# Dilated attention, queries and keys of a head pair: two half-precision parts made before the transpose, and the transpose by DMA instead of by TensorE

## The chip, the cores and the metric

One NeuronCore of a Trainium2 chip runs the whole program. The time is device microseconds of one launch; three timed runs give a median. A separate launch is recorded by the profiler; where the text says "the profiled execution" it means that one.

## The reference, cut to what matters

The program is two layers of an encoder trunk on 1024 tokens of width 1024, in float32. Layer 0 mixes tokens by latent attention, layer 1 by dilated sliding-window attention; each ends in a squared-ReLU MLP. The change is in layer 1:

```
proj = (h @ w_in).reshape(B, S, 3 groups, 3, 16 heads, 64)
for g, (window, dilation) in enumerate(((128, 1), (512, 4), (2048, 16))):
    q = rms_norm(proj[:, :, g, 0], g_q[g]);  k = rms_norm(proj[:, :, g, 1], g_k[g]);  v = proj[:, :, g, 2]
    s = q @ k.T * 64**-0.5 + t5_bias          # only keys inside the dilated window
    o_g, lse_g = softmax(s) @ v, logsumexp(s)
o = sum over g of softmax(lse, axis=g)[g] * o_g
y = o @ w_o
```

## The kernel before, in words

The program is built twice: a fast path (`half` true) that carries each float32 operand as two float16 parts, a rounded high part and the rest, and a float32 path behind an `If` that the data of this case never takes. All that follows is the fast path. A product of two such operands is three float16 matmuls, high by high, high by low and low by high (lines 532 to 534, in `mm3`).

The dilated stage is the function `dil`. Its work is a list of 96 steps, one for each (group g, head pair pr, token-tile pair tp): 3 groups, 8 pairs of heads, 4 pairs of 128-token tiles. Eight head pairs of four steps make a group. Within a group the tokens are permuted so that a dilated window is a plain band, and when the group changes (`turn`) the permuted activations `hTp` are made by copies that are spread over the three elementwise engines (`permute`).

A step n does, in this order of the program:

- `attend` for two token tiles that are ready: `products` (line 2345) multiplies the transposed queries by the transposed keys into two PSUM banks `pss`, twelve matmuls for two tiles; `scores` adds the bias and takes the maximum on VectorE (line 2366) and the exponential on ScalarE (line 2372); the probabilities are split into two float16 parts `ph`, the high by ScalarE (line 2409), the low by VectorE for the first tile and GpSimd for the second (line 2410); then one transposing DMA on SyncE's queue turns `ph` into `pT` (line 2411), 16 blocks of 128x128 in groups 0 and 1 and 8 in group 2.
- `project`: 48 matmuls of 128x256 make queries and keys of the head pair for 256 tokens, in the bank `psproj` (lines 532 to 534).
- between the two halves of `project`, `stacks` for the queries and keys of the step two before: four float32 transposes on TensorE (line 2316) from the normed tile `qn` into a bank `psq`, then the high part by ScalarE (line 2321) and the low part by VectorE (line 2322) from PSUM into `kT`.
- `av`: probabilities by values for the tiles whose `pT` was asked for a step earlier (lines 2424 and 2425), and VectorE's reduction into `U` (line 2432).
- `qkstep`: square (ScalarE, line 2295), sum (VectorE, line 2296), the inverse root (lines 132 to 136), its fourth power on GpSimd for a later check of ranges (lines 2300 to 2302), the scaling out of PSUM into the tile `qn` on VectorE (line 2305) and the gain on the query columns on GpSimd (line 2307).

So the queries and keys of step n are normed at the end of n and the start of n+1, transposed in n+2, and first read by `products` in n+3. `kT` holds for one head pair two planes, high and low, each of 1024 key columns and 512 columns that serve as a ring of four query tiles.

SyncE's queue carries in order, besides the transposes, the weights of the next head pairs (`wqkr`, line 1968), the values (`vraw`), the bias (`bt`), and the stores of `U`. Every engine works its own list in order. The order within an engine's list is set when the program is built: a scheduler places the instructions, and matmuls keep the order of the code. PSUM has eight banks for the stage, handed out in turn. `kT` has two buffers, `qn` shares a pool of four.

The names `P`, `S` are 128 and 1024. These are the functions that the diff touches and what calls them:

Of the kernel before, what the change touches and what calls it, by code (L numbers as in the profile page):

```python
# [9 lines left out]
F32 = mybir.dt.float32  # L10
F32R = mybir.dt.float32r
F16 = mybir.dt.float16
BF16 = mybir.dt.bfloat16
I32 = mybir.dt.int32
AF = mybir.ActivationFunctionType
ALU = mybir.AluOpType
# [4 lines left out]
P = 128  # L21
D = 1024
S = 1024
# [18 lines left out]
class K:  # L42
# [2148 lines left out]
    def dil(self, at0, at1, tail, wqk, vd):  # L2191


        nc, a, tc = self.nc, self.a, self.tc
# [5 lines left out]
        D_ = lambda name, shape, dt, bufs: dpool.tile(list(shape), dt, tag=name, bufs=bufs, name=self.nm(name))  # L2200
# [88 lines left out]
        def qkstep(u, tp, ps):  # L2289

            g = u["g"]
            p8 = ps.rearrange("p (n e) -> p n e", e=64)
            sq = self.T("dsq")
            ms = self.sm("dms", 8)
            nc.scalar.activation(sq, ps, AF.Square, scale=0.125)
            nc.vector.tensor_reduce(ms, sq.rearrange("p (n e) -> p n e", e=64), op=ALU.add, axis=AX.X)
            r = self.rstd(ms, 8, "dr", self.half)
            if self.half:
                y4 = self.sm("y4", 8)
                nc.gpsimd.tensor_tensor(y4, r, r, op=ALU.mult)  # L2300
                nc.gpsimd.tensor_tensor(y4, y4, y4, op=ALU.mult)  # L2301
                nc.gpsimd.tensor_tensor(most, most, y4, op=ALU.add)
            qn = self.T("qn")
            q8 = qn.rearrange("p (n e) -> p n e", e=64)
            nc.vector.tensor_tensor(q8, p8, r.unsqueeze(2).broadcast_to([P, 8, 64]), op=ALU.mult)
            qq = qn.rearrange("p (i n e) -> p i n e", i=2, e=64)[:, :, 0:2, :]
            nc.gpsimd.tensor_tensor(qq, qq, gain[:, g : g + 1, :].unsqueeze(1).broadcast_to([P, 2, 2, 64]), op=ALU.mult)
            return qn

        def stacks(u, tp, qn):  # L2310

            ps = PS("psq")
            for k in range(2):
                for i in range(2):
                    c = i * 256 + (1 - k) * P
                    nc.tensor.transpose(ps[:, (2 * k + i) * P : (2 * k + i + 1) * P], qn[:, c : c + P], self.ident)
            s1 = 4 + tp % 2
            hi, lo = (u["k"][:, k, :].rearrange("p (s x) -> p s x", x=256)[:, tp : s1 + 1 : s1 - tp, :] for k in range(2))
            x = ps.rearrange("p (k x) -> p k x", k=2)
            if self.half:  # L2320
                nc.scalar.activation(hi, x, AF.Copy, scale=64.0)
                nc.vector.scalar_tensor_tensor(lo, x, 64.0, hi, op0=ALU.mult, op1=ALU.subtract)
            else:
                nc.scalar.activation(hi, x, AF.Copy)
                nc.vector.tensor_tensor(lo, x, hi.bitcast(F32), op=ALU.subtract)
            for i in range(2):
                c = S + (tp % 2 * 2 + i) * P
                u["q"][2 * tp + i] = u["k"][:, :, c : c + P]
# [7 lines left out]
        def window(g, t):  # L2336
            return t // 2 * 256 if g == 2 else min(max(P * t - 64, 0), S - 256)

        def products(u, t, pss, i):
            w0 = window(u["g"], t)  # L2340
            q = u["q"].pop(t)
            for n, (a, b) in enumerate(((0, 0), (1, 0), (0, 1))):
                for e in range(2):
                    r = slice(64 * e, 64 * e + 64)
                    nc.tensor.matmul(pss[e][:, i * 256 : (i + 1) * 256], q[r, a, :], u["k"][r, b, w0 : w0 + 256],
                                     start=n == 0, stop=n == 2)

        def bias_load(u, t=0):
# [196 lines left out]
        end = max(n for n, x in enumerate(steps) if x is not None)  # L2545
# [10 lines left out]
        def fetch(n):  # L2556
            for f in wtodo.pop(n, ()):
                f()

        def fetch_split(n):  # L2560
            if n in loads:
                self.held(lambda: wts.update({firsts[n][0:3]: loads.pop(n)()}))
# [51 lines left out]
        transposed, scored, ready, carry, stacking, stk, late = [], [], [], [], None, [], []  # L2614
# [6 lines left out]
        for n, step in enumerate(steps):  # L2621
# [10 lines left out]
            if step is not None:  # L2632
                kind, g, pr, tp = step
                w = wts[(kind, g, pr)]
                if tp == 0:
                    units[(g, pr)] = {"g": g, "pr": pr, "q": {}, "V": VSs[(g, pr // 2)],
                                      "k": D_("kT", (P, 2, S + 512), self.DT, 2), "U": self.G("U", (P, 8, P), F32)}
                u = units[(g, pr)]
            if self.half and step is not None and tp == 0:
                bias_load(u)  # L2640
            fetch_split(n + 1)
            transposed, scored = scored, attend(ready, n > end) if ready else []
            fetch(n)
            for u_, t_, _ in scored:
                if u_["g"] == 2:
# [5 lines left out]
            if turn:  # L2651
# [3 lines left out]
                ps = ahead.pop(0)  # L2655
            elif step is not None and ahead:
                ps = ahead.pop(0)
            elif step is not None:
                ps = PS("psproj")
# [4 lines left out]
            if len(stk) > 1:  # L2664
                x = stk.pop(0)
# [24 lines left out]
            stacking = None  # L2690
            if step is not None:
                stacking = (u, tp, qkstep(u, tp, ps))
# [200 lines left out]
```

## Time and profile before

| | us |
|---|---|
| three timed runs | 3007.45, 3010.37, 3010.95 |
| their median | 3010.37 |
| the profiled execution, its own time | 3005.26 |
| its span, first to last instruction | 3003.1 |

The profiled execution is 5.1 us below the median of the three timed runs, and 2.2 us of its time lie outside the span. The dilated stage goes from about 1548 us to about 2330 us of the span; group 0 ends near 1785, group 1 near 2043. The program also has latent attention and an MLP ahead of the stage, and an output projection and an MLP behind it, which the change leaves as they are.

How to read the rows that the prediction quotes. In a row of a timeline stand start and duration in us, the engine, the line of the program, the operation, tiles written and read, shapes and a count; what stands in brackets is idle time of the engine just before, and what ended it. PE is TensorE's matmul, PEld its weight load, DVE VectorE, ACT ScalarE, POOL GpSimd, SPq SyncE's queue of DMA issues. A matmul's duration includes its pipeline, so what a group of matmuls costs is read from start to start. In a row of the table by windows stand the length of the window, then for each engine its busy time and count, then the granted clock, the mean busy share of the 16 DMA engines and GB/s; the share can pass 1 in a short window, where packets overlap.

### The profile page before, as it was taken

The page shows a single profiled execution, that of the slowest core. Times are in us where ns is not written, and L with a number is a line of the kernel's source. Part 1 is how long each engine was busy: PE and PEld are TensorE (multiplying, and loading weights), DVE is VectorE, ACT ScalarE, POOL GpSimd, SP SyncE. Part 2 cuts the span into 40 slices and gives each one's busy share as a digit, 9 for nine tenths or more (in the row PEclk, how much of TensorE's full clock was granted, in tenths as well). Part 3 has the DMA queues.
Part 4 walks back from the last instruction along what each step waited for, and adds up shares of the span by engine and source line. Part 5 has one row for each costly group of instructions (what it writes and reads, how often), then busy time and mean ns, then how long its engine had stood idle before and what let it go on. Part 6 is the DMA issues. An engine that isn't in the chain of part 4 may idle for free. (4 is left out here: it accounts for less than half of the span.)

```text
span 3003.1 us, 54490 instructions
## 1 busy us (share of the span) xinstructions
PE 2827.4 (94%) x20148; PEld 1676.0 (56%) x20148; DVE 2251.4 (75%) x4902; ACT 1684.2 (56%) x3491; POOL 922.6 (31%) x1276
## 2 busy tenths in 40 slices
PE   6878999999999999999999989998998989999998
PEld 5634566544444444444468878876875434444443
DVE  5687777658988966788768877776886699779565
ACT  4677888825455534533238777775664355555341
POOL 6578888700211000000123344453552002110010
PEclk9999999999999999999999999999999999999999
DMA  6267455425654799546436666565656555457763
GB/s 209 72 169 161 94 117 101 131 84 188 235 188 168 251 278 289 199 159 225 171 116 148 146 139 165 145 128 117 150 129 171 144 191 210 158 186 248 238 196 86
DMA packets 589680, 503.08 MB, mean 168 GB/s; under 512 B 292277, under 2 KB 482018, under 8 KB 589402
## 3 DMA queue, kind: packets, MB, share of 16 engines
q1 hardware_dynamic: 553722, 400.74, 47.9%
q0 software_dynamic: 25248, 87.22, 7.9%
q10 hardware_dynamic: 10432, 11.54, 1.6%
q8 instruction: 159, 2.61, 0.4%
q14 instruction: 119, 0.97, 0.1%
HBM read 317.40 MB, written 125.12 MB: 147 GB/s over the span
## 5 line engine op out<-in xcount | busy, mean ns | idle before, releaser
L534 PE MATMUL psm<-hf,wf 128*128 128x512 f16 x896 | 335.8, 381 | 11.1 <-DVE wf L161 11.1
L532 PE MATMUL psm<-hf,wf 128*128 128x512 f16 x896 | 341.0, 381 | 5.0 <-ACT wf L156 5.0
L533 PE MATMUL psm<-d,d 128*128 128x512 f16 x896 | 340.8, 381 | 4.7 <-DVE d L161 4.7
L534 PE MATMUL psm<-d,d 128*128 128x512 f16 x896 | 340.7, 380 | 0.0
L533 PE MATMUL psm<-hf,wf 128*128 128x512 f16 x896 | 340.6, 380 | 0.0
L532 PE MATMUL psm<-d,d 128*128 128x512 f16 x896 | 335.0, 380 | 0.3 <-ACT d L156 0.3
L1276 POOL TENSOR_TENSOR pp<-p,pp 128x1024 f16<-128x1024 f32 x125 | 275.4, 2209 | 57.9 <-ACT pp L1269 47.8
L532 PE MATMUL psproj<-wqk,hTp 128*128 128x256 f16 x1024 | 283.0, 276 | 0.0
L533 PE MATMUL psproj<-wqk,hTp 128*128 128x256 f16 x1024 | 282.3, 276 | 0.0
L534 PE MATMUL psproj<-wqk,hTp 128*128 128x256 f16 x1024 | 282.0, 275 | 0.0
L156 ACT ACTIVATE d<-ufr 128x1024 f16<-128x1024 f32 x112 | 117.8, 1052 | 211.3 <-PE psm L534 173.3
L897 DVE TENSOR_REDUCE mx<-pmx 128x1 f32<-128x512 f32 x240 | 162.8, 687 | 78.8 <-PE pmx L895 77.4
L161 DVE SCALAR_TENSOR_TENSOR d<-ufr,d 128x1024 f16<-128x1024 f32 x112 | 136.5, 1219 | 76.5 <-ACT d L156 76.4
L1268 ACT ACTIVATE p<-pss 128x512 f32<-128x512 f32 x256 | 149.9, 590 | 43.2 <-PE pss L1259 41.8
L2372 ACT ACTIVATE pd<-pd,dnb 128x192 f32<-128x192 f32 (+2 forms) x384 | 167.3, 437 | 4.1 <-POOL y L2301 2.3
L534 PEld LDWEIGHTS <-wf 128*128 128x128 f16 x896 | 87.8, 98 | 123.3 <-DVE wf L161 19.2
L532 PEld LDWEIGHTS <-wf 128*128 128x128 f16 x896 | 87.9, 98 | 112.9 <-ACT wf L156 10.9
L534 PEld LDWEIGHTS <-d 128*128 128x128 f16 x896 | 87.9, 98 | 111.0 <-issue 6.4
L532 PEld LDWEIGHTS <-d 128*128 128x128 f16 x896 | 88.0, 98 | 106.3 <-issue 2.2
L533 PEld LDWEIGHTS <-d 128*128 128x128 f16 x896 | 87.9, 98 | 106.4 <-issue 2.5
L2410 POOL TENSOR_TENSOR ph<-pd,ph 128x512 f16<-128x512 f32 (+1 forms) x121 | 113.3, 942 | 109.3 <-ACT ph L2409 109.1
L533 PEld LDWEIGHTS <-wf 128*128 128x128 f16 x896 | 88.0, 98 | 104.9 <-issue 1.8
(439 smaller groups left out, 8122.2 us busy)
## 6 DMA issues: line engine op xcount, KB each, us to landing
ufr<-uf SPq DMA_DIRECT2D x112, 512.0 KB
w2r<-in_mlp_w SPq DMA_DIRECT2D x96, 512.0 KB
adaw<-in_ada_w SPq DMA_DIRECT2D x80, 512.0 KB
w1r<-in_mlp_w SPq DMA_DIRECT2D x64, 512.0 KB
wqkr<-in_dil_w_in SPq DMA_DIRECT2D x96, 256.0 KB
wvr<-in_dil_w_in SPq DMA_DIRECT2D x34, 512.0 KB
uf<-ub POOLq DMA_DIRECT2D x32, 512.0 KB, 3.8
uf<-ua POOLq DMA_DIRECT2D x32, 512.0 KB, 3.3
```

The lines of the kernel that those rows point to most:

```text
L156: nc.scalar.activation(hi, src, AF.Copy, scale=scale)
L161: return nc.vector.scalar_tensor_tensor(lo, src, scale, hi, op0=ALU.mult, op1=ALU.subtract, accum_out=self.seen[:, self.nseen - 1 : self.n ...
L532: mm(out, lh, rh, start=first, stop=False)
L533: mm(out, lh, rl, start=False, stop=False)
L534: mm(out, ll, rh, start=False, stop=last)
L897: nc.vector.tensor_reduce(maxes[h][:, 2 * j + b : 2 * j + b + 1], ps, op=ALU.max, axis=AX.X)
L1268: nc.scalar.activation(p[:, b * 512 : (b + 1) * 512], ps[b], AF.Exp, scale=1.0 / self.ss)
L1276: eng.tensor_tensor(q[:, 1], p, q[:, 0], op=ALU.subtract)
L2372: nc.scalar.activation(p[:, e, lo:hi], p[:, e, lo:hi], AF.Exp, scale=1.0 / self.ss, bias=nb[:, e : e + 1], accum_out=stat[:, g, t, 1, 2 * ...
L2410: (nc.gpsimd if i or u["g"] == 2 else nc.vector).tensor_tensor(lo, p, hi, op=ALU.subtract)
```

## The change

On the fast path the two parts are made where the tokens are still on the partitions, and the transpose is done on float16 by DMA:

- a new function `turned` takes the normed tile `qn` of the step just before: ScalarE copies it to float16 (line 2319 of the kernel after), GpSimd subtracts to get the low part (line 2320), both into a new tile `hl` of two buffers, whose four blocks for a token tile are query high, query low, key high, key low; then SyncE's queue issues one transposing DMA for each of the two token tiles, four blocks of 128x128 each (line 2323), straight into `kT`.
- `kT` now has four planes of 1024 columns (query high, query low, key high, key low), for all tokens of the head pair; `products` reads queries and keys from it by plane.
- the factor 64 that was applied at the two evictions moves into the scaling out of PSUM, which becomes a scalar-tensor-tensor operation in place of a tensor-tensor one.
- `stacks` does nothing for a step that was turned. The last two of the 96 steps are not turned: they keep the transposes on TensorE and the evictions.

```
+            rb = r.unsqueeze(2).broadcast_to([P, 8, 64])
+            if self.half:
+                nc.vector.scalar_tensor_tensor(q8, p8, 64.0, rb, op0=ALU.mult, op1=ALU.mult)
...
+        def turned(u, tp, qn):
+
+            x = qn.rearrange("p (i s c) -> p i s c", i=2, s=2)
+            hl = D_("hl", (P, 2, 4, P), F16, 2)
+            hi, lo = hl[:, :, 0:3:2], hl[:, :, 1:4:2]
+            nc.scalar.activation(hi, x, AF.Copy)
+            nc.gpsimd.tensor_tensor(lo, x, hi, op=ALU.subtract)
+            for i in range(2):
+                t = 2 * tp + i
+                nc.sync.dma_start_transpose(out=u["k"][:, :, t * P : t * P + P], in_=hl[:, i].rearrange("p a c -> p (a c)"))
...
         def stacks(u, tp, qn):
 
+            if qn is None:
+                return
...
-            if self.half:
-                nc.scalar.activation(hi, x, AF.Copy, scale=64.0)
-                nc.vector.scalar_tensor_tensor(lo, x, 64.0, hi, op0=ALU.mult, op1=ALU.subtract)
...
+            k = u["k"]
+            q, k = (k[:, 0:2, t * P : t * P + P], k[:, 2:4]) if self.half else (u["q"].pop(t), k)
...
-                                      "k": D_("kT", (P, 2, S + 512), self.DT, 2), "U": self.G("U", (P, 8, P), F32)}
+                                      "k": D_("kT", (P, 4, S), F16, 2) if self.half else D_("kT", (P, 2, S + 512), self.DT, 2), "U": self.G("U", (P, 8, P), F32)}
...
             transposed, scored = scored, attend(ready, n > end) if ready else []
+            if self.half and stacking is not None and n < end:
+                turned(*stacking)
+                stacking = stacking[:2] + (None,)
```

How the instructions stand now. On SyncE's queue, a piece from group 0 before:

```order
L2411 DMA_TRANSPOSE pT_17745<-ph_17744 128x16x128
L2448 DMA U<-U_16636 128x8x128
L1968 DMA wqkr_17897<-in_dil_w_in 128x4x128
L2411 DMA_TRANSPOSE pT_17877<-ph_17876 128x16x128
L2411 DMA_TRANSPOSE pT_18012<-ph_18011 128x16x128
```

The same place of the queue after; `hl_17880` and `hl_18013` are the parts of two steps that follow each other:

```order
L2467 DMA U<-U_16637 128x8x128
L1968 DMA wqkr_17885<-in_dil_w_in 128x4x128
L2323 DMA_TRANSPOSE kT_17711<-hl_17880 128x4x128
L2430 DMA_TRANSPOSE pT_17860<-ph_17859 128x16x128
L2323 DMA_TRANSPOSE kT_17711<-hl_17880 128x4x128
L2323 DMA_TRANSPOSE kT_17711<-hl_18013 128x4x128
L2430 DMA_TRANSPOSE pT_17993<-ph_17992 128x16x128
L2323 DMA_TRANSPOSE kT_17711<-hl_18013 128x4x128
```

Every step now has two more transposing DMAs; in many steps one of them stands ahead of the transposing DMA of the probabilities and one behind it.

On ScalarE, one step of group 0 before (the second `ph`, the eviction between the two, and the square of the next step):

```order
L2409 ACTIVATE ph_18846<-pd_18848 128x512
L2372 ACTIVATE pd_18857,stat<-pd_18857,dnb_18860 128x256 x2
L2321 ACTIVATE kT_18274<-psq_18893 128x2x256
L2409 ACTIVATE ph_18846<-pd_18857 128x512
L2295 ACTIVATE dsq_18945<-psproj_18868 128x512
```

And after:

```order
L2428 ACTIVATE ph_18815<-pd_18817 128x512
L2319 ACTIVATE hl_18836<-qn_18785 128x4x128
L2428 ACTIVATE ph_18815<-pd_18826 128x512
L2295 ACTIVATE dsq_18912<-psproj_18842 128x512
```

The copy into `hl` stands where the eviction of `psq` stood, between the two `ph`; what it reads is the tile `qn` of the step just before, where the eviction read one that is a step older.

On GpSimd, one step of group 0 before:

```order
L2302 TENSOR_TENSOR most<-most,y_3008_18812 128x8
L2307 TENSOR_TENSOR qn_18816<-qn_18816,dgain 128x2x128
L2410 TENSOR_TENSOR ph_18846<-pd_18857,ph_18846 128x512
L2300 TENSOR_TENSOR y_3033_18957<-dry_18949 128x8
L2301 TENSOR_TENSOR y_3033_18957<-y_3033_18957 128x8
```

And after:

```order
L2302 TENSOR_TENSOR most<-most,y_3009_18781 128x8
L2311 TENSOR_TENSOR qn_18785<-qn_18785,dgain 128x2x128
L2320 TENSOR_TENSOR hl_18836<-qn_18785,hl_18836 128x4x128
L2429 TENSOR_TENSOR ph_18815<-pd_18826,ph_18815 128x512
L2300 TENSOR_TENSOR y_3034_18924<-dry_18916 128x8
```

The new subtraction stands between the gain and the low part of the second `ph`; in some steps it stands behind that low part instead.

More of the change, by code (lines that the diff above doesn't have):

```diff
@@ L2304, in qkstep @@
             q8 = qn.rearrange("p (n e) -> p n e", e=64)
-            nc.vector.tensor_tensor(q8, p8, r.unsqueeze(2).broadcast_to([P, 8, 64]), op=ALU.mult)
+            rb = r.unsqueeze(2).broadcast_to([P, 8, 64])
+            if self.half:
+                nc.vector.scalar_tensor_tensor(q8, p8, 64.0, rb, op0=ALU.mult, op1=ALU.mult)
+            else:
+                nc.vector.tensor_tensor(q8, p8, rb, op=ALU.mult)
             qq = qn.rearrange("p (i n e) -> p i n e", i=2, e=64)[:, :, 0:2, :]
@@ L2314, in stacks @@
                 for i in range(2):
-                    c = i * 256 + (1 - k) * P
+                    c = i * 256 + (k if self.half else 1 - k) * P
                     nc.tensor.transpose(ps[:, (2 * k + i) * P : (2 * k + i + 1) * P], qn[:, c : c + P], self.ident)
+            if self.half:
+                x, kq = ps.rearrange("p (k x) -> p k x", k=2), u["k"][:, :, tp * 256 : tp * 256 + 256]
+                nc.scalar.activation(kq[:, 0:3:2], x, AF.Copy)
+                nc.vector.tensor_tensor(kq[:, 1:4:2], x, kq[:, 0:3:2], op=ALU.subtract)
+                return
             s1 = 4 + tp % 2
@@ L2319, in stacks @@
             x = ps.rearrange("p (k x) -> p k x", k=2)
-            if self.half:
[L2321 to L2325, printed above, removed]
+            nc.scalar.activation(hi, x, AF.Copy)
+            nc.vector.tensor_tensor(lo, x, hi.bitcast(F32), op=ALU.subtract)
             for i in range(2):
@@ L2340, in products @@
             w0 = window(u["g"], t)
-            q = u["q"].pop(t)
+            k = u["k"]
+            q, k = (k[:, 0:2, t * P : t * P + P], k[:, 2:4]) if self.half else (u["q"].pop(t), k)
             for n, (a, b) in enumerate(((0, 0), (1, 0), (0, 1))):
@@ L2344, in products @@
                     r = slice(64 * e, 64 * e + 64)
-                    nc.tensor.matmul(pss[e][:, i * 256 : (i + 1) * 256], q[r, a, :], u["k"][r, b, w0 : w0 + 256],
+                    nc.tensor.matmul(pss[e][:, i * 256 : (i + 1) * 256], q[r, a, :], k[r, b, w0 : w0 + 256],
                                      start=n == 0, stop=n == 2)
```

## The prediction

> **What bounds the kernel now.** I read the page's busy shares first, then the dilated stage by windows, TensorE's waits inside that stage, and single steps in the timeline. The page:
>
> ```profile
> span 3003.1 us, 54490 instructions
> PE 2827.4 (94%) x20148; PEld 1676.0 (56%) x20148; DVE 2251.4 (75%) x4902; ACT 1684.2 (56%) x3491; POOL 922.6 (31%) x1276
> ```
>
> TensorE is the bound of the whole program. The change lies in the stage from 1548 to 2330 us, so what counts is whether TensorE bounds there too. The windows for groups 0, 1 and 2, and for all of the stage:
>
> ```profile
> 1548.00:1800.00 252.00, 242.54 (x2622) 209.86 (x2620) 199.85 (x640) 195.74 (x569) 98.21 (x197) 0.99 0.59 135
> 1800.00:2043.00 243.00, 227.47 (x2461) 196.63 (x2459) 178.79 (x611) 179.48 (x549) 103.65 (x233) 0.98 0.61 142
> 2043.00:2300.00 257.00, 225.04 (x2239) 189.68 (x2238) 203.82 (x663) 158.11 (x537) 123.39 (x212) 0.97 0.65 144
> 1548.00:2330.00 782.00, 721.12 (x7487) 610.13 (x7485) 601.18 (x1977) 547.59 (x1698) 325.96 (x641) 0.98 0.61 141
> ```
>
> TensorE is busy 721 of 782 us; VectorE (601) and ScalarE (548) follow at a distance, GpSimd (326) is far off, the DMA engines are at 0.61. What ends TensorE's idle time in this stage, its matmuls first, then the row for weight loads on the same cause, then the rows of group 2 alone (2043 to 2330):
>
> ```profile
> PE psav L2424 <- DMA pT<-ph: 25.0, 12, 6.2
> PE pss L2345 <- DVE kT L2322: 14.8, 12, 2.8
> PE pss L2345 <- ACT kT L2321: 7.8, 10, 1.8
> PE psq L2316 <- POOL qn L2307: 5.8, 1, 5.8
> PE psq L2316 <- DVE qn L2305: 2.9, 2, 2.4
> PEld L2424 <- DMA pT<-ph: 29.8, 17, 6.5
> PE pss L2345 <- DVE kT L2322: 8.5, 9, 1.7
> PE pss L2345 <- ACT kT L2321: 6.0, 9, 1.6
> ```
>
> So there are two kinds of wait: for the transposed probabilities (17 times), and for the two evictions into `kT` (22 times, 22.6 us). In light steps there is none. Two successive groups of the transposes in question, group 0:
>
> ```profile
> 1649.17 0.60 PE L2316 MATMUL psq<-ident,qn 128*128 128x128 f32 x4
> 1656.39 0.60 PE L2316 MATMUL psq<-ident,qn 128*128 128x128 f32 x4
> ```
>
> The step is 7.22 us, and TensorE works through it without a pause.
>
> **What leaves TensorE.** Cost from start to start:
>
> ```profile
> 1766.06 0.27 PE L534 MATMUL psproj<-wqk,hs 128*128 128x256 f16 x1
> 1766.17 0.60 PE L2316 MATMUL psq<-ident,qn 128*128 128x128 f32 x4
> 1766.61 0.27 PE L532 MATMUL psproj<-wqk,hT 128*128 128x256 f16 x1
> ```
>
> The four transposes hold TensorE from 1766.17 to 1766.61, 0.44 us. 94 of the 96 steps lose them: 94 x 0.44 = 41.4 us. All of it lies on the path, as TensorE has no pause in a light step; what is late next is weighed below. The 22.6 us of waits for `kT` go too, since no eviction stands between transposes and products any more. The wait of 5.8 us is that of the last steps, which keep their transposes, so it stays; the 2.9 us I leave as they are, since the late VectorE behind them stays late for the scores.
>
> **What moves between engines.** Durations of the removed and the nearest kept operations, and of the transposing DMAs:
>
> ```profile
> L2321 ACT ACTIVATE kT<-psq x96: 569/574/598, 1549.6 to 2317.2; 128x512 f16<-128x512 f32 x96
> L2322 DVE SCALAR_TENSOR_TENSOR kT<-psq,kT x96: 671/688/693, 1550.2 to 2318.8; 128x512 f16<-128x512 f32 x96
> L2409 ACT ACTIVATE ph<-pd x186: 398/614/632, 1557.4 to 2283.6; 128x512 f16<-128x512 f32 x128, 128x256 f16<-128x256 f32 x58
> L2410 POOL TENSOR_TENSOR ph<-pd,ph x121: 663/1152/1607, 1565.1 to 2289.7; 128x512 f16<-128x512 f32 x63, 128x256 f16<-128x256 f32 x58
> L2411 SPq DMA_TRANSPOSE pT<-ph x93: 1232/1599/4400, 1559.2 to 2290.4; - x93
> L842 SPq DMA_TRANSPOSE k<-qkv x32: 1238/1297/2550, 197.8 to 529.8; - x32
> ```
>
> VectorE loses 94 x 0.688 = 64.7 us. Its scaling into `qn` becomes another form on the same shape; the removed eviction at 0.688 us has that form on that shape, so I count no change. ScalarE exchanges a copy of 0.574 us for one like the `ph` copy, 0.614 us: 3.8 us more in all, beside its waits. GpSimd gains 94 x 1.152 = 108 us, from 326 to 434 of some 745 us: not a bound.
>
> SyncE's queue gains 188 issues. Four blocks to a transfer do not occur before. The nearest rows are the 8-block transfers of group 2 and of the attention in layer 0, at least 1.24 us of issue, and I take that, since the fixed part shows in the minimum of both; if the issue grew with blocks alone it would be 0.4 us (1.6 / 4), and under a full queue up to 4.4. Per step that makes 2.5 us more on a queue that now issues some 3 us in a step of 6.8. What an issue of this kind waits for is new: SyncE waits for `hl` from GpSimd, and behind it stand the transposing DMA of the probabilities, weights, bias and stores of `U`.
>
> The data: the first window is the transfer of one 16-block transposing DMA, the second the whole light step around it.
>
> ```profile
> 1655.18:1657.29 2.11, 2.11 (x22) 1.93 (x20) 1.54 (x8) 1.79 (x7) 0.95 (x4) 1.00 1.20 279
> 1645.78:1653.00 7.22, 7.22 (x83) 6.34 (x82) 5.99 (x21) 6.05 (x19) 2.69 (x6) 1.00 0.54 112
> ```
>
> 16 blocks take 2.11 us of transfer, so 8 blocks in a step take 1.06 us and each four-block DMA 0.53. In share: 2.11 x 1.20 / 2 = 1.27 us of all engines; the step had 0.54 x 7.22 = 3.9 and gets 5.2 of 6.78, 0.76. Over the stage 0.61 becomes about 0.83: busier queues, no bound.
>
> **The new waits.** In the light step of group 0:
>
> ```profile
> 1650.76 0.73 POOL L2307 TENSOR_TENSOR qn<-qn,dgain 128x256 f32<-128x256 f32 x1
> 1651.65 0.57 ACT L2321 ACTIVATE kT<-psq 128x512 f16<-128x512 f32 x1
> 1652.12 0.62 ACT L2409 ACTIVATE ph<-pd 128x512 f16<-128x512 f32 x1
> 1652.82 1.16 POOL L2410 TENSOR_TENSOR ph<-pd,ph 128x512 f16<-128x512 f32 x1 [1.33 <-ACT ph L2409]
> ```
>
> The copy into `hl` takes the place of the eviction at 1651.65 and needs the gain, which ends at 1651.49: it just fits. If it is late, the second `ph` and the next square wait behind it on ScalarE. GpSimd then subtracts from about 1652.2 to 1653.4, so the low part of `ph` starts near 1653.4 in place of 1652.82: 0.6 us later. Against that VectorE's list is 0.69 us shorter between `ph` and the sums that start the next step, so I net the two to nothing. One four-block transfer stands ahead of the probabilities' one and takes 0.53 us of the DMA engines; its issue (1.24 us) runs while GpSimd makes the last part (1.16 us). So I take the probabilities to be 0.5 us later, between 0 (all hidden) and 3.5 us (both new issues, 2.48, and the data, 1.06, ahead). Products read `kT` two steps after `hl` is asked for; from the gain's end at 1651.49 to a landing there are about 0.6 + 1.2 + 1.2 + 2 = 5 us against a step and a half. In group 2, where VectorE and GpSimd also merge, I leave a third of the 14.5 us of waits for `kT` in place: 5 us come back.
>
> **What is late next.** The path from products to probabilities, in a light step, and one wait that shows what a transposing DMA needs from issue to use:
>
> ```profile
> 1645.78 0.83 PE L2345 MATMUL pss<-kT 64*128 64x256 f16 x12
> 1654.00 1.64 SPq L2411 DMA_TRANSPOSE pT<-ph  x1
> 1659.45 0.22 PE L2424 MATMUL psav<-vs,pT 128*128 128x128 f16 x1
> 2008.25 1.60 SPq L2411 DMA_TRANSPOSE pT<-ph  x1
> 2011.94 0.29 PE L2424 MATMUL psav<-vs,pT 128*128 128x128 f16 x1 [2.71 <-DMA pT<-ph]
> ```
>
> Issue is 8.22 us after the products, use possible 3.69 us later: 11.9 us. TensorE comes to it after 13.67 us, so 1.76 us are to spare. Between the two lie two groups of transposes, so TensorE will come 0.88 us sooner; with the probabilities 0.5 us later 0.4 us are left. Light steps stay bound by TensorE at 6.78 us. Where TensorE waits already nothing is to spare: each of the 17 waits grows by 0.88 + 0.5 = 1.38 us, 23.5 us given back.
>
> **The sum.** 41.4 + 22.6 - 23.5 - 5 = 35.5 us. Against the profiled execution (span 3003.1, time 3005.3) that gives 2969.8. The three timed runs lie higher, median 3010.37; from there 2975, which I predict.
>
> **The rivals.** (1) *All of it counts.* VectorE's relief of 0.69 us a step shortens the late steps, and the 17 waits don't grow: 41.4 + 22.6 = 64 us, 2946. For it: the waits fall in steps where VectorE also splits weights or copies. Against it: the second `ph` now queues behind the new subtraction. (2) *The probabilities become the bound.* Products two steps on cannot start before 11.9 us, plus 0.77 us for `av` (1659.45 to 1660.22, where the products of two steps later stand), plus the delay d: a step is at least 6.34 + d/2. At d = 0.88 this meets 6.78, at d = 1.76 the old 7.22. With d near 1.7 the 64 steps of groups 0 and 1 gain nothing, group 2 gains 30 x 0.44 + 9.5 = 23 us, and the 17 waits take about 20: 3007. For it: SyncE's queue is in order. (3) *Slower: SyncE's queue and the DMA engines hold up the probabilities.* With both new transfers ahead, d = 3.5 us and a step 8.1 us: 64 x 0.88 = 56 us lost, less the 23 of group 2, 3043; it is slower from d above about 2. Against it, four 8-block transfers in a row in layer 0, in issue, and the DMA engines while they move:
>
> ```profile
> 310.83 2.91 SPq L842 DMA_TRANSPOSE q<-qkv  x2
> 313.85 2.58 SPq L842 DMA_TRANSPOSE k<-qkv  x2
> 312.92:318.20 5.28, 4.17 (x57) 2.45 (x54) 4.94 (x6) 3.57 (x5) 3.06 (x2) 1.00 1.14 228
> ```
>
> They follow each other at 1.3 to 1.5 us and their data move without a gap, so transposing DMAs overlap. This rival has a rule behind it: the Trainium skill, page "VectorE: DVE Perf Modes", sections "The three transpose paths" and "Rules for kernel authors", takes TensorE for a 128x128 transpose wherever PSUM will do as a destination, and gives 390 ns there against 1309 ns by DMA. By those figures eight blocks would take some 10.5 us of each step, an estimate from that page that is longer than the step. The trace disagrees for blocks in one transfer, 16 in 2.11 us.
>
> **How the numbers follow.** The forecast has 0.56; rival 1, 0.16; rival 2, 0.16, half of it within 0.2%; rival 3, 0.12. A measurement of this kernel tells about 0.2%, 6 us, from no change. Faster: 0.56 + 0.16 + 0.08 = 0.80; same 0.08; slower 0.12. The forecast's own range is 2955 to 2992 (the 17 waits growing by 0.2 to 2.4 us each). The range of 2938 to 3008 takes in rival 1 with some of the 25 us of present waits gone, and half of rival 2.
>
> **What would show it.** Right: in the profile after, a light step of group 0 lasts 6.78 us; TensorE's waits for `kT` are gone or a few us, on DMA now; its waits for `pT` rise from 25 to between 35 and 50 us; VectorE is busy some 65 us less, GpSimd 108 us more; four-block issues take about 1.2 us. Wrong: light steps of 7.0 us or more with a wait for `pT` in each (rivals 2 and 3); products that wait for DMA `kT`; GpSimd late in group 2, seen as SyncE's waits for `hl`.

## The result, and the profile after

The changed kernel takes 3049.57 us (median of 4 runs, 3048.32 to 3050.05) against 3008.91 us for the kernel before (median of 4, 3007.22 to 3010.95): a ratio of 1.0134, 95% interval 1.0117 to 1.0152. It is slower by 41 us where the prediction had it faster by 35. The profiled execution took 3049.22 us. Its page:

```profile
span 3047.3 us, 54068 instructions
PE 2816.0 (92%) x19772; PEld 1649.2 (54%) x19772; DVE 2222.8 (73%) x4808; ACT 1687.4 (55%) x3491; POOL 1031.2 (34%) x1370
```

TensorE's busy time fell by only 11 us although 94 x 0.44 = 41 us of transposes are gone: something stretches what is left. The table by windows, one row a group (from the group's first product to that of the next), of the kernel before and then of the kernel after:

```profile
1552.00:1795.00 243.00, 233.54 (x2536) 202.00 (x2536) 192.68 (x616) 190.19 (x553) 95.10 (x189) 0.99 0.59 136
1795.00:2048.00 253.00, 237.27 (x2564) 205.09 (x2562) 186.16 (x640) 186.83 (x572) 106.66 (x240) 0.98 0.62 143
2048.00:2321.00 273.00, 240.27 (x2316) 196.31 (x2312) 212.95 (x692) 162.39 (x553) 122.37 (x207) 0.97 0.64 148
```

```profile
1554.00:1810.00 256.00, 229.35 (x2404) 191.63 (x2405) 184.11 (x586) 191.92 (x559) 133.98 (x223) 0.96 0.77 168
1810.00:2079.00 269.00, 232.53 (x2431) 193.67 (x2431) 178.55 (x613) 189.65 (x575) 143.36 (x275) 0.95 0.77 166
2079.00:2371.00 292.00, 239.35 (x2208) 190.73 (x2205) 201.01 (x655) 159.89 (x545) 155.17 (x234) 0.91 0.77 159
```

Every group is longer, by 13, 16 and 19 us, with fewer matmuls in it, and the granted clock, the last figure but two, is lower in each. What ended TensorE's idle time in the stage:

```profile
PE pss L2364 <- DMA kT<-hl: 59.2, 30, 8.1
PE psav L2443 <- DMA pT<-ph: 50.1, 27, 5.8
```

The waits for `kT` have not gone, they have grown from 22.6 to 59.2 us and are now on the transfer; those for `pT` have doubled from 25.0. By group the waits for `kT` are 8.9, 8.0 and 42.3 us, and those for `pT` 18.9, 28.5 and 2.7. Yet a step without a wait is what the prediction made of it. Products of two successive light steps:

```profile
1699.31 0.83 PE L2364 MATMUL pss<-kT 64*128 64x256 f16 x12
1706.09 0.83 PE L2364 MATMUL pss<-kT 64*128 64x256 f16 x12
```

That is 6.78 us, but only 16 of the 32 steps of group 0 last 6.9 us or less, 9 of group 1 and 6 of group 2. How a `kT` tile comes late shows in one step of group 1, here the timeline of GpSimd, ScalarE and SyncE's queue, then of the products that read the tile:

```profile
1946.85 0.89 POOL L2311 TENSOR_TENSOR qn<-qn,dgain 128x256 f32<-128x256 f32 x1
1947.70 1.15 POOL L2429 TENSOR_TENSOR ph<-pd,ph 128x512 f16<-128x512 f32 x1
1947.77 0.63 ACT L2319 ACTIVATE hl<-qn 128x512 f16<-128x512 f32 x1 [0.88 <-POOL qn L2311]
1948.82 1.15 POOL L2320 TENSOR_TENSOR hl<-qn,hl 128x512 f16<-128x512 f32 x1
1948.88 3.21 SPq L2430 DMA_TRANSPOSE pT<-ph  x1
1952.19 2.52 SPq L2323 DMA_TRANSPOSE kT<-hl  x2
1955.85 0.50 PE L2364 MATMUL pss<-kT 64*128 64x256 f16 x6 [0.42 <-DMA kT<-hl]
```

ScalarE stands 0.88 us for the gain, GpSimd takes `ph` first, the low part ends at 1949.97, and then `kT` waits 2.2 us more for the issue of `pT` ahead of it in SyncE's queue. From the gain's end at 1947.74 to the products 8.1 us pass, and they still wait 0.42.

In group 2 another thing is late. The windows of a pause that a `kT` tile caused, of the burst behind it and of the stretch that follows:

```profile
2137.00:2141.40 4.40, 0.00 (x0) 0.00 (x0) 1.18 (x3) 1.93 (x5) 2.36 (x3) 1.00 1.20 169
2141.40:2142.00 0.60, 0.55 (x11) 0.58 (x12) 0.00 (x0) 0.00 (x0) 0.00 (x0) 1.00 1.13 193
2142.00:2145.40 3.40, 3.40 (x21) 2.14 (x16) 2.22 (x15) 2.24 (x12) 1.25 (x4) 0.50 1.23 242
```

TensorE does nothing for 4.4 us while the DMA engines are fully taken (share 1.20), and 0.6 us after it starts again the granted clock is 0.50 for 3.4 us: the pause is paid again in part. The issues around it:

```profile
2131.05 1.13 SPq L1968 DMA_DIRECT2D wqkr<-in_dil_w_in  x2
2132.34 3.15 SPq L2323 DMA_TRANSPOSE kT<-hl  x2
2130.46 0.58 ACTq L2554 DMA_DIRECT2D um<-U  x1
2131.14 1.28 ACTq L2545 DMA_DIRECT2D oTd<-oT  x2
2132.58 0.62 ACTq L2554 DMA_DIRECT2D um<-U  x1
2135.73 0.61 ACTq L2554 DMA_DIRECT2D um<-U  x1
2141.45 0.96 PE L2364 MATMUL pss<-kT 64*128 64x256 f16 x12 [4.58 <-DMA kT<-hl]
```

Both `kT` transfers are issued by 2135.49, and the products wait to 2141.45. Two weight loads, three loads of `um` and two stores of `oT`, 256 KB each, are issued within some 5 us around them; they share the engines with `kT`. It is so throughout group 2: the ten `kT` transfers that landed more than 7 us after their issue each had four or more issues of `um` and `oT` within 4 us of their own, and the other 47 landed in 2.3 to 6.3 us (read from the completion counts of the transfers).

### The profile page after: what moved, and what is told of

Read it like the earlier page. It is cut to its first block, busy times and chain, and to the rows that moved or that the text cites. A ratio compares the mean times of both kernels' runs of the same rounds, so it can differ in the third digit from the quotient of the medians.

```text
span 3047.3 us, 54068 instructions
## 1 busy us (share of the span) xinstructions
PE 2816.0 (92%) x19772; PEld 1649.2 (54%) x19772; DVE 2222.8 (73%) x4808; ACT 1687.4 (55%) x3491; POOL 1031.2 (34%) x1370
## 5 line engine op out<-in xcount | busy, mean ns | idle before, releaser
L532 PE MATMUL psproj<-wqk,hTp 128*128 128x256 f16 x1024 | 290.1, 283 | 0.0
L533 PE MATMUL psproj<-wqk,hTp 128*128 128x256 f16 x1024 | 289.2, 282 | 0.1
L534 PE MATMUL psproj<-wqk,hTp 128*128 128x256 f16 x1024 | 288.6, 282 | 0.0
L534 PEld LDWEIGHTS <-wf 128*128 128x128 f16 x896 | 87.8, 98 | 121.4 <-DVE wf L161 17.4
L271 DVE SCALAR_TENSOR_TENSOR adacc<-adaw,cond,adacc 128x1024 f32<-128x1024 f32 (+1 forms) x98 | 126.3, 1289 | 32.9 <-DMA adaw<-in_ada_w 32.0
L2385 DVE CUSTOM_DVE_ANT_0 pd<-pss,bt 128x192 f32<-128x192 f32 (+2 forms) x384 | 114.7, 345 | 47.0 <-PE pss L2364 45.5
L532 PEld LDWEIGHTS <-wf 128*128 128x128 f16 x896 | 87.8, 98 | 112.8 <-ACT wf L156 10.8
L534 PEld LDWEIGHTS <-d 128*128 128x128 f16 x896 | 87.9, 98 | 110.8 <-issue 6.1
L2364 PE MATMUL pss<-kT 64*128 64x256 f16 x1152 | 91.0, 291 | 61.5 <-DMA kT<-hl 59.2
L2451 DVE TENSOR_REDUCE U<-psav 128x128 f32<-128x256 f32 x192 | 76.1, 418 | 96.2 <-PE psav L2444 96.2
```

The source lines that it names most:

```text
L271: return self.nc.vector.scalar_tensor_tensor(acc, w, c, acc, op0=ALU.mult, op1=ALU.add)
L532: mm(out, lh, rh, start=first, stop=False)
L533: mm(out, lh, rl, start=False, stop=False)
L534: mm(out, ll, rh, start=False, stop=last)
L2385: nc.vector.tensor_tensor_reduce(p[:, e, lo:hi], pss[e][:, i * 256 + lo - off : i * 256 + hi - off], bt[:, e, lo - b0 : hi - b0], op0=ALU. ...
```

## The experiments

I had three theories. *Late kT*: the chain from `qn` over two engines and SyncE's queue takes longer than the program leaves for it. *The queue* (rival 3 of the prediction): SyncE's issues and the DMA engines hold up the probabilities. *The chain of the parts*: making `hl` on ScalarE and GpSimd holds up the probabilities, whatever is transferred. All kernels were timed beside the kernel before, which took 3005 to 3009 us in these comparisons, so the ratios are what to compare. Lengths of groups are from the first products of one to those of the next, group 2's to its last product; waits are those of TensorE's matmuls for `kT` (the one that TensorE turns itself, or the DMA's) and for `pT`; clock is that granted from 1548 to 2378 us.

| kernel | us | ratio to before, 95% | groups 0, 1, 2, us | waits kT / pT, us | clock |
|---|---|---|---|---|---|
| before | 3008.9 | | 242.8, 252.9, 273.3 | 22.6 / 25.0 | 0.98 |
| after | 3049.6 | 1.0117 to 1.0152 | 255.6, 269.4, 291.6 | 59.2 / 50.1 | 0.94 |
| e1 layout alone | 3007.0 | 0.9991 to 1.0014 | 243.6, 255.6, 270.6 | 21.4 / 24.7 | 0.98 |
| e2 parts, unread | 3039.5 | 1.0092 to 1.0132 | 257.2, 258.9, 286.4 | 34.1 / 31.0 | 0.96 |
| e3 transfers, unread | 3043.7 | 1.0104 to 1.0138 | 262.8, 266.6, 284.0 | 24.1 / 54.3 | 0.96 |
| e4 products later | 3041.8 | 1.0107 to 1.0141 | 252.3, 262.1, 283.9 | 1.3 / 90.6 | 0.93 |
| e5 as e2, hl behind ph | 3023.8 | 1.0042 to 1.0077 | 253.6, 252.6, 285.6 | 31.7 / 24.0 | 0.97 |
| e6 as e4, hl behind ph | 3035.0 | 1.0084 to 1.0119 | 252.9, 264.7, 279.1 | 1.3 / 96.1 | 0.93 |
| e7 as e6, av later | 3004.3 | 0.9987 to 1.0006 | 231.9, 253.1, 277.4 | 8.0 / 25.2 | 0.95 |
| e8 before, av later | 2999.1 | 0.9968 to 0.9987 | 241.1, 245.7, 277.9 | 37.8 / 0 | 0.96 |
| e9 after, hl behind ph | 3051.3 | 1.0132 to 1.0166 | 255.8, 262.8, 292.1 | 50.8 / 49.3 | 0.94 |
| e10 after, av later | 3056.1 | 1.0149 to 1.0190 | 254.5, 263.2, 302.0 | 113.8 / 0 | 0.93 |
| e11 as e7, low part on VectorE | 3013.8 | 1.0016 to 1.0035 | 242.4, 247.0, 279.0 | 14.3 / 20.2 | 0.96 |
| e12 a form for each group | 2986.2 | 0.9916 to 0.9949 | 231.3, 244.6, 268.6 | 21.1 / 22.2 | 0.98 |
| e13 after, SyncE in code order | 3084.8 | 1.0247 to 1.0281 | 267.4, 269.4, 307.6 | 35.2 / 44.0 | 0.93 |
| e14 after, weights from ScalarE | 3078.6 | 1.0230 to 1.0271 | 268.2, 273.5, 294.9 | 54.8 / 69.5 | 0.93 |
| e15 before, av later in 0 and 1 | 2988.0 | 0.9929 to 0.9964 | 240.2, 244.2, 268.7 | 28.8 / 8.8 | 0.98 |
| e16 after, low part on VectorE | 3064.6 | 1.0174 to 1.0210 | 262.9, 266.0, 301.6 | 59.2 / 49.2 | 0.92 |

### e1: the layout alone

```
-            if self.half and stacking is not None and n < end:
+            if False:
```

> Every step of the stage turns its q and k on TensorE again; what stays of the change is the layout of kT and the one fused VectorE instruction for qn. All three theories (the kT tiles land too late; SyncE's queue and the DMA engines hold up the probabilities; the ScalarE-GpSimd chain is too long) put the loss into the transfer or what feeds it, so all expect the time of before: 3009 us, give or take 6. A time above 3020 would mean that the layout or the fused instruction costs something by itself.

Measured 3007.0 us, no difference. The planes of `kT` and the fused scaling cost at most 4 us (the end of the interval); the loss is in the parts and their transfer.

### e2 and e5: the parts made and not read, and their place in the queues

In e2 TensorE turns all tiles, and the parts are made beside it:

```
-                stacking = stacking[:2] + (None,)
...
-                nc.sync.dma_start_transpose(out=u["k"][:, :, t * P : t * P + P], in_=hl[:, i].rearrange("p a c -> p (a c)"))
```

> Every step turns q and k on TensorE and uses those; the halves hl are made as well, on ScalarE and GpSimd, and nothing reads them (work added, nothing removed, no transfer). Theory of the late kT: 3009 to 3016 us, since no product waits for hl. Theory of the queue: the same, 3009 to 3016. Theory of the chain (ScalarE waiting for GpSimd's gain ahead of hl, GpSimd's hl ahead of ph): probabilities are held up as in the changed kernel, 3030 us or more, with the waits of av for pT at 50 us or more in the stage.

Measured 3039.5 us. With no transfer and no reader 34 us are lost: the chain theory had said so, the other two had not. Its sign in the waits did not come, though: those for `pT` are 31.0 us, where it wanted 50 or more. Where it comes from, in the timeline of e2, ScalarE, GpSimd and SyncE in a step of group 0:

```profile
1706.70 0.62 ACT L2319 ACTIVATE hl<-qn 128x512 f16<-128x512 f32 x1
1707.22 0.62 ACT L2425 ACTIVATE ph<-pd 128x512 f16<-128x512 f32 x1
1707.40 1.16 POOL L2320 TENSOR_TENSOR hl<-qn,hl 128x512 f16<-128x512 f32 x1 [1.32 <-ACT hl L2319]
1708.52 1.16 POOL L2426 TENSOR_TENSOR ph<-pd,ph 128x512 f16<-128x512 f32 x1
1709.70 1.65 SPq L2427 DMA_TRANSPOSE pT<-ph  x1
```

On both engines `hl` stands ahead of `ph`: 0.52 us on ScalarE, and on GpSimd the subtraction for `ph` could start at 1707.8 and starts at 1708.52. The issue of `pT` comes a median of 9.50 us after the products in group 0, where it was 8.13 before. e5 ties `hl` behind `ph` on both:

```
-            nc.scalar.activation(hi, x, AF.Copy)
-            nc.gpsimd.tensor_tensor(lo, x, hi, op=ALU.subtract)
+            self.behind(lambda: nc.scalar.activation(hi, x, AF.Copy), mybir.EngineType.Activation)
+            self.behind(lambda: nc.gpsimd.tensor_tensor(lo, x, hi, op=ALU.subtract), mybir.EngineType.Pool)
```

> As the run with hl made and not read (3039.5 us), with one thing moved: on ScalarE and on GpSimd hl's instruction is tied behind the step's copies and low parts of ph. Theory of the place in the queues (hl standing ahead of ph holds each probability tile up by some 0.5 us on ScalarE and 0.6 us on GpSimd): the time falls back to 3008 to 3018 us and the median from the products to the issue of pT goes from 9.5 to about 8.1 us in group 0. Rival, the work itself (0.6 us of ScalarE and 1.16 us of GpSimd a step lengthen the norm of the next q and k wherever hl stands): 3028 to 3040 us.

Measured 3023.8 us, between the two. The issue of `pT` still comes a median of 9.07 us after the products in group 0, where 8.1 was expected; in group 1 it comes after 7.90 (7.76 in the kernel before). The order is as meant:

```profile
1704.15 0.62 ACT L2436 ACTIVATE ph<-pd 128x512 f16<-128x512 f32 x1
1704.67 0.62 ACT L2330 ACTIVATE hl<-qn 128x512 f16<-128x512 f32 x1
1704.86 1.16 POOL L2437 TENSOR_TENSOR ph<-pd,ph 128x512 f16<-128x512 f32 x1 [1.32 <-ACT ph L2436]
1705.97 1.16 POOL L2331 TENSOR_TENSOR hl<-qn,hl 128x512 f16<-128x512 f32 x1
```

So in this kernel the place of `hl` costs 16 us (the ratio falls from 1.0112 to 1.0060) and the work itself 18 us. Neither is in the waits for `pT` alone: in e2 these rose by 6 us, the waits for TensorE's own `kT` by 11, and the clock fell from 0.98 to 0.96, which by an estimate is 0.02 x 830 = 17 us.

### e3: the transfers as well

```
+                sink = D_("sink", (P, 4, P), F16, 2)
-                nc.sync.dma_start_transpose(out=u["k"][:, :, t * P : t * P + P], in_=hl[:, i].rearrange("p a c -> p (a c)"))
+                nc.sync.dma_start_transpose(out=sink, in_=hl[:, i].rearrange("p a c -> p (a c)"))
```

> As the run with hl made and not read, and now the two transposing transfers of four blocks a step are issued on SyncE too, into tiles that nobody reads; TensorE's own transposes feed the products. Theory of the late kT: no product waits, so at most 3010 to 3022 us. Theory of the queue: the probabilities are issued and land as late as in the changed kernel, and the time is 3050 us or more (the 41 us of TensorE's transposes are still paid), with av's waits for pT at 100 us or more. Theory of the chain: the same as the run without the transfers.

Measured 3043.7 us, a ratio of 1.0121 after e2's 1.0112: 3 us, with intervals that overlap. The waits for `pT` do rise, from 31.0 to 54.3 us, but those for `kT` fall by 10, and little is left in the time. All 188 transfers are issued, and in the window of the stage the DMA share, the last figure but one, is 0.77 in place of 0.59 in e2:

```profile
1548.00:2378.00 830.00, 744.67 (x7506) 619.01 (x7505) 627.05 (x1983) 594.35 (x1793) 432.55 (x736) 0.96 0.77 164
```

The theory of the queue, with 3050 us or more, falls. Now the kernel after is e3 without TensorE's 41.4 us, and its ratio is not lower but 0.0013, 4 us, higher: the step from `kT` turned by TensorE to `kT` that comes by DMA takes back about 45 us.

### e4, e6, e9, e10, e7: slack for one tile, or for both

e4 takes the products up a step later, e10 the product with the values; e6 and e9 are e4 and the changed kernel with `hl` behind `ph`; e7 has both slacks and `hl` behind `ph`.

```
-            if len(stk) > 1:
+            if len(stk) > (2 if self.half else 1):
```

```
-            transposed, scored = scored, attend(ready, n > end) if ready else []
+            now = attend(ready, n > end) if ready else []
+            transposed, waiting, scored = (waiting, scored, now) if self.half else (scored, [], now)
```

> The changed kernel with the products taken up one step later (and one step more at the end of the stage), so that a kT tile has about two and a half steps from its q and k to its products. Theory of the late kT: the products' waits for kT (59 us in the stage) and the half-clock spells behind them go, and the time falls to 2975 to 3000 us. Theory of the queue: the waits for kT go, but the probabilities are issued as late as now; 3030 to 3050 us, with av's waits for pT unchanged at 50 us on PE. Theory of the chain: as the queue's, 3030 us or more, with ScalarE's 37 us of waiting for GpSimd still there.

Measured 3041.8 us. In e4 no product waits for the DMA's `kT` any more; nearly all of TensorE's waits in the stage are now

```profile
PE psav L2443 <- DMA pT<-ph: 90.6, 33, 8.3
```

The theory of the late `kT`, taken alone, falls as well: 59 us of waits went and 40 came at the other tile, and the clock is 0.93.

> The changed kernel with the products one step later (3041.8 us as it was) and hl tied behind ph on ScalarE and GpSimd. Theory of the place in the queues: with kT's slack given, the only loss left was the delay of the probabilities, so this run keeps TensorE's 41 us and is at 2975 to 3000 us. Rival, the work itself: 3025 to 3040 us. Rival, the transfers (SyncE alternates kT and pT, the DMA engines are 0.78 busy): 3010 to 3030 us, with av's waits for pT still over 60 us.

Measured 3035.0 us: the order may help by 7 us here, with intervals that overlap, and the waits for `pT` stay at 96.1. The theory of the place falls; the time is that of the rival of the work itself, the waits are those of the rival of the transfers.

> The changed kernel (3050 us) with hl tied behind ph on ScalarE and GpSimd, nothing else. Theory that both tiles are late: the probabilities are issued up to a microsecond earlier and kT about a microsecond later, so one wait grows as the other shrinks; 3040 to 3055 us, with the products' waits for kT above 59 us. The on-record rival (only the probabilities are held up): 3015 to 3030 us.

Measured 3051.3 us, no change, as expected of two late tiles; the waits for `kT` fell, though, which I had expected to rise. So the 16 us that the place of `hl` cost in e2 are not to be had in the changed kernel by the order alone.

> The changed kernel with only av one step later (three pT tiles), so that the probabilities have a step of slack and kT has none. Theory that kT's lateness costs by itself: the waits for pT go, those of the products for kT stay at 55 us or grow, and the time is at 3020 to 3045 us. The on-record rival (the probabilities): 2985 to 3005 us.

Measured 3056.1 us, above what either theory gave. With a step of slack for the probabilities nearly all of TensorE's waiting is

```profile
PE pss L2364 <- DMA kT<-hl: 113.8, 46, 7.7
```

The two sums belong together: 59.2 + 50.1 = 109.3 in the kernel after, 113.8 with slack for `pT`, 90.6 with slack for `kT`. Each chain by itself is too long for the step; to shorten one gives TensorE's pause to the other.

> As the run before in this list, and av is taken up one step later too (three pT tiles, one step more at the end), so that neither kT nor pT has to be on time within a step. Every theory that puts the loss into lateness (of kT, of pT, by whatever queue) expects TensorE to run through: the waits for kT and pT under 15 us in the stage, the half-clock spells down to 30 us or fewer, and 2955 to 2975 us. If the engines that make q and k are the bound (VectorE, ScalarE or GpSimd work per step above 6.8 us), the steps stay at 7.2 us and more and the time is at 2990 to 3020 us.

The run before in that list is e6. Measured 3004.3 us: by the ratios 41 us below the kernel after, and level with the one before. The waits for the two tiles are down from 109 to 33 us, where under 15 had been expected:

```profile
PE psav L2454 <- DMA pT<-ph: 25.2, 15, 4.7
PE pss L2375 <- DMA kT<-hl: 7.6, 10, 1.9
```

So lateness of the two tiles was the cause of the loss: against e9, the same order without the slacks, e7 is 46 us faster. But the 41 us of TensorE's work that the change took away did not become a gain: group 0 is 11 us shorter than before, group 1 the same, group 2 four longer, the clock in the stage is 0.95, and the time is far above the 2955 to 2975 that I had written. It lies in the range of the other answer, 2990 to 3020 us, which held if the engines that make queries and keys are the bound. In group 0, with the DMA engines busy for 0.91 of the time, most steps are 6.8 us:

```profile
1557.00:1789.00 232.00, 220.83 (x2387) 187.84 (x2385) 179.91 (x579) 185.05 (x541) 127.34 (x216) 0.98 0.91 182
```

That answer also wanted steps of 7.2 us and more, which group 0 does not have. What holds groups 1 and 2 I have not settled. The trace shows that TensorE now waits for other things, which VectorE makes:

```profile
PE pss L2375 <- DVE qn L2318: 12.3, 3, 10.9
PE psproj L543 <- DVE stat L2396: 8.4, 5, 3.2
PE psproj L544 <- DVE wqk L161: 6.9, 7, 1.6
```

### e8: the kernel before with the later av

> The kernel before, with TensorE's transposes, and only av taken up one step later (three pT tiles, one step more at the end). What the prediction priced as the waits for pT (25 us in the stage, of which 23.5 should grow by the shorter step) is gone: 2975 to 2995 us if those waits and the half clock behind them are real losses (25 us and up to 15 us of clock), 3000 to 3010 if something else takes their place at once.

The edit is the second one above, on the kernel before. Measured 2999.1 us (0.9968 to 0.9987). The 25 us of waits for `pT` are gone and group 1 gains 7 us, but the waits for `kT` rise from 22.6 to 37.8 and group 2 loses 5: nearest to the second answer that I had written.

### e11 and e16: the low part on VectorE

```
-            nc.gpsimd.tensor_tensor(lo, x, hi, op=ALU.subtract)
+            nc.vector.tensor_tensor(lo, x, hi, op=ALU.subtract)
```

> The changed kernel with hl's low part on VectorE (0.7 us) instead of GpSimd (1.16 us, and 108 us in all). If GpSimd's part of the chain makes kT and pT late, 3015 to 3035 us; if VectorE's 5.7 us of work in a 6.8 us step and the transfers do, 3045 to 3060 us.

> The run with both slacks and hl behind ph (3004 us), with hl's low part on VectorE (about 0.7 us a step there) instead of GpSimd (1.16 us). If GpSimd's added 108 us are what still disturbs steps there, 2980 to 2995 us; if VectorE's work sets them (it then has its 65 us back), 3005 to 3020 us; within 3 us of 3004 if neither does and the transfers' landings do.

Measured 3064.6 us on the changed kernel and 3013.8 us on e7. By the ratios they are worse by 17 and 9 us: taking the part from GpSimd does not make the tiles earlier (59.2 and 49.2 us of waits in e16, as in the kernel after). VectorE's time counts: e11 is in the range written for VectorE's work as the bound. Group 1 alone gains in e11, 247.0 against 253.1.

### e13 and e14: SyncE's queue

```
                     self.pin_from(mark, mybir.EngineType.PE)
+                    self.pin_from(mark, mybir.EngineType.SP)
```

> The changed kernel (3050 us) with SyncE's list in the order of the code: the probabilities' transpose of a step, then both of kT, where the scheduler had put it between the two in many steps. If the place of the second kT transfer behind pT is what makes kT late, 3015 to 3035 us and under 30 us of waits for kT; if the elementwise chain ahead of the transfers does, 3040 to 3060 us.

Measured 3084.8 us. The waits for `kT` did shrink, from 59.2 to 35.2 us. That does not show that the place behind `pT` made them late: in this run the tiles land 0.6 to 0.7 us later after their gain than in the kernel after (medians of groups 0 and 1). TensorE comes to the products later too, by 1.1 us in group 0, since the weights now stand in that order too and new waits come in:

```profile
PE psav L2443 <- DMA pT<-ph: 44.0, 29, 4.7
PE pss L2364 <- DMA kT<-hl: 35.2, 29, 5.2
PE psproj L533 <- DVE wqk L161: 19.5, 18, 2.5
```

```
-                loads[n] = self.dil_weights(g, pr, parts=parts)
+                loads[n] = self.dil_weights(g, pr, parts=parts, eng=nc.scalar)
```

> The changed kernel with the stage's weight loads (wqkr) issued from ScalarE instead of SyncE. If SyncE's queue makes kT and pT late, 3020 to 3035 us; if the chain of elementwise work does, 3045 us or more, since ScalarE, which is in that chain, now issues four loads more for every four steps; if the DMA engines' load itself does, no change (3044 to 3056 us), since the same bytes move.

Measured 3078.6 us. With the weights' loads off SyncE TensorE waits no less: 54.8 us for `kT`, and 69.5 for `pT`, 19 more than in the kernel after. ScalarE, which now issues the loads, is in both chains, so the run does not clear SyncE's queue; it shows only that moving the loads there does not help.

### e12 and e15: a version that beats both

e12 gives each group the form that was shortest for it (group 0: the change with both slacks and the order; group 1: TensorE's transposes and the later av; group 2: as before). e15 is the kernel before with the later av in groups 0 and 1 only, so without the change:

```
+            transposed, waiting, scored = (waiting, scored, now) if self.half and step is not None and step[1] < 2 else (waiting + scored, [], now)
```

> Each group of the stage in the form that was shortest for it: group 0 with the change, its products and av one step later and hl behind ph; group 1 with TensorE's transposes and av one step later; group 2 as before the change. From the groups' times in those runs, 231.9, 245.7 and 273.3 us against 242.8, 252.9 and 273.3 before, the sum is 18 us under before: 2985 to 2995 us. If what a group gains is given back at the borders between the forms, 2997 to 3010 us.

> The kernel before with av one step later in groups 0 and 1 only. The best version (2986 us) without the change in group 0: if group 0 owes its 231 us there to the change, this run's group 0 is at 241 us and the time at 2993 to 2999 us; if the later av alone gave it, 2984 to 2989 us.

Measured 2986.2 and 2988.0 us. Both beat both kernels, and the sum of groups was right for e12, but the two cannot be told apart. Group 0 of e12 and then of e15, by windows:

```profile
1560.00:1791.00 231.00, 215.78 (x2342) 184.18 (x2343) 177.37 (x573) 184.44 (x542) 123.58 (x213) 0.97 0.89 182
```

```profile
1551.00:1792.00 241.00, 233.01 (x2527) 202.43 (x2526) 193.79 (x614) 190.29 (x553) 93.83 (x190) 0.99 0.61 135
```

Group 0 does owe 9 us to the change, but its first products come 8 us later (1559.5 against 1551.4), since the longer pipeline starts a step later. They end at the same place. What makes the kernel faster is one more step for the probabilities in groups 0 and 1; the transposes by DMA add nothing that I could measure.

## Why the prediction was wrong

- **The light step, right.** 6.78 us, as worked out; the four-block issue took a median of 1.26 us (1.24 was taken), GpSimd 108.6 us more (108), and the waits for `pT` rose to 50 (35 to 50). But half of the steps or more are not light.
- **"From the gain's end at 1651.49 to a landing there are about 0.6 + 1.2 + 1.2 + 2 = 5 us against a step and a half": this step failed.** In the trace of the kernel after the median from the end of the gain to the last packet of the second transfer is 7.75 us in group 0 and about 8.5 in group 1, and up to 14. The parts of the sum were each about right (0.62, 1.16, 1.26 and a landing 2.0 after the issue); it left out what stands between them: ScalarE behind the gain or an exponential, GpSimd behind `ph`, a second issue, and the issue of `pT` ahead of it. And a step and a half was not there: in the trace of before, products start a median of 9.6 us after the gain, at steps of 7.22; with two groups of transposes less between them that is 8.7 us, an estimate from these rows. A need of about 8 with a spread of several us against 8.7 is late in many steps. So 22.6 us of waits were counted as gone and 59.2 were there.
- **"So I net the two to nothing", and d = 0.5: failed.** The issue of `pT` came 1.15 us (group 0) and 1.76 us (group 1) later after its products. Made and read by nobody, the parts cost 34 us (e2), of which e5 puts 16 on their place ahead of `ph`; the prediction had them at half a microsecond of delay.
- **"Busier queues, no bound": wrong in group 2.** The share was 0.77, below the 0.83 forecast (which the prediction's own terms don't give: 0.61 x 782 + 94 x 1.27 over 745 us is 0.80), and in groups 0 and 1 landings took 2 us; but 42 of the 59 us of waits for `kT` are in group 2, where the mean hides stretches at 1.20 in which loads and transposes share the engines. That the loads of `um` and the stores of `oT` are the cause there is read from the trace; no run took them away.
- **The clock was in no term.** It fell from 0.98 to 0.94 in the stage: 0.04 x 830 = 33 us by an estimate. Beside it stand 62 us more of waits for the two tiles (109.3 against 47.6) and 41 us less of transposes; together that is 54 us where the result is 41, so the terms overlap in part. The clock goes with TensorE's pauses: 0.98 in the kernel before, e1, e12 and e15, 0.92 to 0.94 in all runs whose waits for the two tiles come to over 79 us; e7 has 0.95 with 33 us of these waits, and the others that are shown there. The Trainium skill, page "TensorE: Matmul & The Clock Gate", section "Why this matters for your kernels", says to leave no idle gap above some 3 us between bursts of matmuls, as the clock then falls to half; the pause of 4.4 us shown above agrees. Here shorter pauses were followed by it too, as one of 2.47 us in group 0, with the window that begins 0.8 us behind it:

```profile
1752.09 0.50 PE L2364 MATMUL pss<-kT 64*128 64x256 f16 x6 [2.47 <-DMA kT<-hl]
1752.90:1756.31 3.41, 3.41 (x19) 2.35 (x17) 2.57 (x13) 2.40 (x9) 1.53 (x5) 0.50 1.01 242
```

- **VectorE -65 us: -29.** The evictions did go; a part of what came in their place, 9 us in one group of instructions, is in the last section.
- **Rival 3 had nearly the time and not the cause.** It gave 3043 us from light steps of 8.1 us with the probabilities 3.5 us late. Light steps are 6.78 and the delay is 1.2 to 1.8; in e3 the transfers cost 3 us, and in e10 a whole step more for the probabilities brought nothing. The rule of the Trainium skill that stood beside it (page "VectorE: DVE Perf Modes", section "Rules for kernel authors": TensorE for a transpose wherever PSUM will do) gives the right advice here, but its price for a block does not show: four blocks were issued in 1.26 us and landed 2.0 us after the issue began.

The account from the runs, by their ratios: parts made, +34 us (e2), 16 of them by their place (e5); transfers, +3 (e3); TensorE's transposes gone, -41; and the rest, about +45, when products read the `kT` that comes by DMA. The rest is what the other terms leave of the 41 us that the change costs, and no run measures it alone. What shows that it is lateness, and of both tiles, is that slack for either one (e4, e6, e10) brings little or nothing and slack for both (e7) wins 46 us against e9; some 7 us of that the same slack for `pT` also gives the kernel before (e8).

## What to carry to other kernels

Before work is taken off the engine that bounds, follow the tile that the new path makes from its last input to its first reader, with every instruction and issue that stands ahead of it in each in-order queue, and compare that, with its spread, with the time to the reader in the shorter step; if they are close, the bound engine will wait, and here its clock fell on top. When two tiles are due in the same step, slack for one only moves the pause to the other: give both a step, and first try that step without the change, since here it was worth more than the change.

## What the runs showed of the hardware

A small VectorE instruction can last as long as a GpSimd one that started just before it. GpSimd's low part and VectorE's step of the root in the kernel after:

```profile
2051.44 1.15 POOL L2320 TENSOR_TENSOR hl<-qn,hl 128x512 f16<-128x512 f32 x1 [0.30 <-ACT hl L2319]
2051.52 1.09 DVE L134 SCALAR_TENSOR_TENSOR drt<-dms,dry 128x8 f32<-128x8 f32 x1
```

The instruction on 128x8 elements takes 0.16 us as a rule; here it ends with GpSimd's, at 2052.6. Twenty instructions of this tile took 0.6 us or more in the kernel after and two in the one before, each of them ending with a GpSimd instruction that started before it, and they lie in the chain to the next `qn`. By groups of instructions, before and after:

```profile
L134 DVE SCALAR_TENSOR_TENSOR drt<-dms,dry 128x8 f32<-128x8 f32 x95 | 17.1, 180 | 5.5 <-ACT dry L133 5.4
```

```profile
L134 DVE SCALAR_TENSOR_TENSOR drt<-dms,dry 128x8 f32<-128x8 f32 x95 | 26.3, 277 | 12.2 <-ACT dry L133 12.0
```

The mean of the group rose from 180 to 277 ns. The Trainium skill, page "SBUF — State Buffer", section "SBUF: two separate sides", says that VectorE and GpSimd share a port pair by an exclusive lock that is held for a whole instruction; these rows agree.
